# Last product of a two-layer trunk: two of the four weight sums of a pair by DMA accumulation, five pairs by seven products

## The chip, the cores and the metric

The kernel runs on one core of one Trainium2 chip. The metric is the device time of one execution in microseconds. The core has five engines that work side by side, each through its own instruction queue in order: TensorE (PE in the profile, its weight loads PEld), VectorE (DVE), ScalarE (ACT), GpSimd (POOL) and SyncE (SP, which here only issues DMAs). Engines wait for each other by semaphores. A DMA is issued by an engine's queue and done by 16 DMA engines.

## What is computed

Two decoder layers on 256 tokens of 1024 channels. Each layer is a half-weighted SwiGLU block, an attention block and a second half-weighted SwiGLU block; a final RMSNorm closes it. Only the last SwiGLU block of layer 1 and the final norm matter here:

```
def swiglu(h, w_gate, w_up, w_down):
    return (jax.nn.silu(h @ w_gate) * (h @ w_up)) @ w_down
...
h = h + FFN_RESIDUAL_WEIGHT * swiglu(rmsnorm(h, ffn2_norm[layer]),
                                     ffn2_w_gate[layer], ffn2_w_up[layer], ffn2_w_down[layer])
...
return rmsnorm(h, final_norm)
```

`w_down` is 2816 x 1024 in float32. The last product multiplies the activations (256 tokens x 2816) by it.

## The kernel before, in words

Every float32 product is done as three matmuls of a rounded type: each operand is split into a high part (a rounded copy, made by ACT) and a low part (the rest, made by DVE as source minus high part), and `product()` (L181) issues high x high, high x low and low x high, each 128x128 against 128x512, all into one PSUM tile.

The last product is `down_last()` (L435). The 2816 rows of `w_down` are 22 blocks of 128 rows, taken as 11 pairs (0 to 10). For one pair the work is a product of two 2x2 block matrices: two blocks of tokens by two blocks of rows on the left, two blocks of rows by two halves of 512 columns on the right. An ordinary pair takes eight block products (24 matmuls). A pair whose number is in `FAST` (L29, before: 2, 4, 6, 7) takes seven (21 matmuls), by sums of blocks of the left and of the right side. `fast()` (L476) issues them in the order 1, 11, 12, 5, 7, 6, 21; the products 1, 5, 6 and 7 add up over the fast pairs in four PSUM tiles m1, m5, m6, m7, and `collect()` (L486) combines these into the output tiles `h` after the last fast pair: one ACT instruction, six of DVE and two of POOL. The pairs 9 and 10 are kept back (`tail=2`) and done output block by output block, so that each block can be finished (residual added at L524, squares and gain) while PE works on the next.

The weights of a pair come in by `load()` (L459): one DMA of 1 MB from SP's queue into a tile `raw` of four quarters, numbered 0 to 3: first row block, left and right half, then second row block, left and right half. An ordinary pair is split as it is. A fast pair needs four sums of quarters, named a, c, b and d:

- a = quarter 0 + quarter 1 and c = quarter 3 + quarter 1, both by one DVE instruction over 1024 columns into the tile `ac` (L467);
- b = a + quarter 3, by POOL (L468);
- d = b + quarter 2, by POOL (L469).

`split()` (L448) makes high and low parts in four pieces: a (quarters 0 and 2), b (quarter 3), c (the tile `ac`) and d (the sums b and d). In names of the profile `wh_f_d_8c` is the high part of piece c of pair 8, and `wl_f_d_8c` its low part. The sums of the left side of a fast pair are made one stage earlier, in `quarter_sums()` (L342), while that pair's activations are made.

What sets the order and the waits:

- `raw` has four buffers, shared by all loads of weights, so the load of pair i + 4 waits until everyone has read pair i's tile: ACT, DVE and, in a fast pair, POOL.
- The high and the low pieces have eight buffers each (`wp`), so a piece is split only when PE has used the one eight pieces back.
- The tiles `ac` use the tag `qkl` with two buffers, which the attention used before for the low parts of its queries and keys; each fast pair reuses the buffers of the fast pair two back.
- Each engine's order is fixed when the program is built, by a scheduler that places instructions by when it expects their inputs. A wait in a queue holds everything behind it on that engine, DMA issues included.

In the stage before, the gate and up products of the same SwiGLU block, POOL multiplies each `j_f_u` by the norm's row (L371), between DVE's steps L339 and L379.

Of the kernel before, what the change touches and what calls it, by code (L numbers as in the profile page):

```python
# [11 lines left out]
F32R = mybir.dt.float32r  # L12
AF = mybir.ActivationFunctionType
ALU = mybir.AluOpType

P = 128
# [9 lines left out]
NG = H // HG  # L26
ROT = 16
HALF = ROT // 2
FAST = (2, 4, 6, 7)  # L29
LEAD = 4  # L30
EPS = 1e-6
SCALE = DH ** -0.5
# [34 lines left out]
def trunk(ctx: ExitStack, tc: tile.TileContext, a: dict, out: bass.AP):  # L67
    nc = tc.nc
# [7 lines left out]
    pp = ctx.enter_context(tc.tile_pool(name="pp", bufs=2))  # L76
# [101 lines left out]
    def rows(w, k0, k, c0, n):  # L178
        return w[k0 * P:(k0 + k) * P, c0:c0 + n].rearrange("(k p) n -> p k n", p=P)
# [255 lines left out]
    def down_last(name, w, blocks, sums, h, weight, part, after, tail=2):  # L435
# [12 lines left out]
        def split(n, *srcs):  # L448
            k = sum(src.shape[1] for src in srcs)
            wh, wl = [wp.tile([P, k, 512], F32R, tag=tag, name=f"{tag}_{name}_{n}") for tag in ("wh", "wl")]  # L450
            at = 0
            for src in srcs:
                part = slice(at, at + src.shape[1])
                nc.scalar.activation(wh[:, part], src, AF.Copy)
                nc.vector.tensor_sub(wl[:, part], src, wh[:, part].bitcast(F32))
                at = part.stop
            return [(wh[:, i, :], wl[:, i, :]) for i in range(k)]

        def load(i):  # L459
            raw = rawp.tile([P, 4, 512], F32, tag="raw", name=f"raw_{name}_{i}")  # L460
            nc.sync.dma_start(raw.rearrange("p (k c) n -> p k (c n)", k=2), rows(w, 2 * i, 2, 0, D))
            if i not in sums:
                return split(f"{i}a", raw[:, :2]) + split(f"{i}b", raw[:, 2:])
            n = 2 * (sorted(sums).index(i) % 4)
            ac = ap_.tile([P, 2, 512], F32, tag="qkl", name=f"sum_{name}_{i}ac", bufs=2)
            b, d = [xp.tile([P, 1, 512], F32, tag=f"x{n + j}", name=f"sum_{name}_{i}{'bd'[j]}") for j in range(2)]
            nc.vector.tensor_add(ac, raw[:, 0::3], raw[:, 1:2].to_broadcast([P, 2, 512]))  # L467
            nc.gpsimd.tensor_tensor(b[:, 0], ac[:, 0], raw[:, 3], op=ALU.add)  # L468
            nc.gpsimd.tensor_tensor(d[:, 0], b[:, 0], raw[:, 2], op=ALU.add)  # L469
            b11, b21 = split(f"{i}a", raw[:, 0::2])  # L470
            b22, = split(f"{i}b", raw[:, 3:])
            ta, tc = split(f"{i}c", ac)
            tb, td = split(f"{i}d", b, d)
            return b11, b21, b22, ta, tc, tb, td
# [24 lines left out]
        quarters = [[("11", c11), ("12", c12)], [("21", c21), ("22", c22)]]  # L499
        pairs = KF // 2  # L500
        ahead, held = [load(0)], []
        for i in range(pairs):
            if i + 1 < pairs:
                ahead.append(load(i + 1))
            ws = ahead.pop(0)
            if i in sums:
                fast(i, ws)
                if i == max(sums):
                    collect()
            elif i < pairs - tail:  # L510
                for k in range(2):
                    for t in range(NT):
                        for c in range(2):
                            add(*quarters[t][c], blocks[t][2 * i + k], ws[2 * k + c])
            else:
                held += [(2 * i + k, ws[2 * k:2 * k + 2]) for k in range(2)]
        end = acc(f"dn_{name}_end")[:, :S]
        for t in range(NT):
            for c in range(2):
                n, ac = quarters[t][c]  # L520
# [232 lines left out]
    w, n = a["a_w_qkv"][0], HG * DH  # L753
# [25 lines left out]
    sums = {}  # L779
    for n, i in enumerate(FAST):  # L780
        if n < 2:
            sums[i] = tuple(xp.tile([P, 512], F32R, tag=f"kx{4 + 2 * n + j}", name=f"left_{i}_{j}") for j in range(2))
        else:
            parts = ap_.tile([P, 2, 512], F32R, tag="qkh", name=f"left_{i}", bufs=2)
            sums[i] = (parts[:, 0], parts[:, 1])
# [78 lines left out]
```

## Time and profile before

| | us |
|---|---|
| median of three runs | 986.85 (986.69 to 988.29) |
| the profiled execution | 986.84 |
| span of its trace | 985.1 |
| PE busy in the span | 972.6 |
| DVE busy | 753.1 |
| ACT busy | 594.7 |
| POOL busy | 213.1 |
| last product on PE, first to last matmul | 921.5 to 979.0 |

In the rows of a timeline the columns are start and length in us, the engine, the line of the kernel, the operation, output and inputs by the program's names (leading numbers in names are left out), the shape, the count, and in brackets how long the engine stood idle before and which engine's instruction ended that. A group's row gives the least, the median and the longest duration in ns and the first and last start. The matmuls' lengths are modelled; the distance from one start to the next, 0.227 us for 128x512, is what PE takes for each. SPq, ACTq and POOLq are the queues' own instructions, such as DMA issues.

### The profile page before, as it was taken

Reading aid. Unit: us, or ns where it says so; the run is one execution under the profiler, and the core shown is the slowest. Engines: PE = TensorE matmul, PEld = TensorE weight load, DVE = VectorE, ACT = ScalarE, POOL = GpSimd, SP = SyncE. Lnnn points to the kernel's source line nnn. Section 1 sums busy time; section 2 is a strip of 40 time slices with the busy share of each in tenths; the row PEclk is TensorE's granted clock in tenths of the full one; section 3 lists DMA queues with packets and bytes.
Section 4 is the critical chain, followed back from the end, with each engine's and each line's share of the span. In section 5 each row is a group of like instructions: output and inputs, shape, how many; then the busy total and the mean of one; then the engine's idle time right before and its main releaser. Section 6 shows DMA issues by size and latency. Waiting matters only on the chain.

```text
span 985.1 us, 15279 instructions
## 1 busy us (share of the span) xinstructions
PE 972.6 (99%) x5640; PEld 847.2 (86%) x5640; DVE 753.1 (76%) x1313; ACT 594.7 (60%) x1090; POOL 213.1 (22%) x220
## 2 busy tenths in 40 slices
PE   8999999999999999999999999999999999999997
PEld 5888888888889888888888888888888998888886
DVE  7987866677877788776668887657677778888996
ACT  7666654457776665654456556544577766666561
POOL 3211111122332211110112111111042422112461
PEclk9999999999999999999999999999999999999999
DMA  9876565655443556555655565665544255565351
GB/s 317 256 242 208 161 210 186 214 172 166 133 130 107 181 187 203 178 198 189 213 173 172 185 200 184 200 196 192 197 132 140 90 168 164 180 200 184 128 172 43
DMA packets 152251, 176.03 MB, mean 179 GB/s; under 512 B 3440, under 2 KB 140144, under 8 KB 152176
## 3 DMA queue, kind: packets, MB, share of 16 engines
q1 hardware_dynamic: 151328, 174.01, 55.1%
q8 instruction: 44, 0.72, 0.3%
q10 hardware_dynamic: 848, 1.05, 0.3%
q14 instruction: 31, 0.25, 0.1%
HBM read 173.99 MB, written 1.05 MB: 178 GB/s over the span
## 4 chain that ended last, share of the span: by engine, by line
PE 68%; ACT 2%; DVE 2%; issue 1%; POOL 0%; POOLq 0%; ACTq 0%; DVEq 0%
PE f_g L195 12%; PE f_u L195 12%; PE dn_f L195 8%; PE f_u L198 6%; PE f_g L198 6%; PE dn_f L198 4%; PE dn_f_d L184 1%; PE dn_f_d L186 1%; PE dn_f_d L188 1%; PE q_b L184 1%; PE kv_b L184 1%; PE q_b L188 1%; PE kv_b L188 1%; PE q_b L186 1%; PE kv_b L186 1%; PE ot_ao L546 1%
## 5 line engine op out<-in xcount | busy, mean ns | idle before, releaser
L195 PE MATMUL f_g<-x_n,wh_f_g 128*128 128x512 f32 x688 | 180.4, 394 | 0.0
L195 PE MATMUL f_u<-x_n,wh_f_u 128*128 128x512 f32 x688 | 177.3, 390 | 0.0
L371 POOL TENSOR_TENSOR j_f_u<-j_f_u,r_n 128x256 f32<-128x256 f32 x88 | 80.5, 917 | 376.2 <-DVE j_f_u L339 352.7
L195 PEld LDWEIGHTS f_u<-x_n,wh_f_u 128*128 128x128 f32 x688 | 129.2, 188 | 27.3
L195 PEld LDWEIGHTS f_g<-x_n,wh_f_g 128*128 128x128 f32 x688 | 124.0, 189 | 22.7
L195 PE MATMUL dn_f<-act_f,wh_f 128*128 128x512 f32 x528 | 126.5, 391 | 0.0
L159 DVE TENSOR_TENSOR wl_f_u<-raw_f_u,wh_f_u 128x1024 fp32r<-128x1024 f32 x86 | 118.5, 1380 | 2.9 <-ACT wh_f_u L158 2.8
L159 DVE TENSOR_TENSOR wl_f_g<-raw_f_g,wh_f_g 128x1024 fp32r<-128x1024 f32 x86 | 103.5, 1233 | 15.7 <-PE f_g L198 9.3
L195 PEld LDWEIGHTS dn_f<-act_f,wh_f 128*128 128x128 f32 x528 | 96.9, 188 | 18.6
L159 DVE TENSOR_TENSOR wl_f<-raw_f,wh_f 128x1024 fp32r<-128x1024 f32 x72 | 81.8, 1153 | 36.0 <-ACT wh_f L158 26.8
L198 PE MATMUL f_u<-x_n,wl_f_u 128*128 128x256 f32 x688 | 103.3, 283 | 0.0
L198 PE MATMUL f_g<-x_n,wl_f_g 128*128 128x256 f32 x688 | 102.7, 282 | 0.0
L198 PEld LDWEIGHTS f_g<-x_n,wl_f_g 128*128 128x128 f32 x688 | 96.4, 190 | 6.2
L158 ACT ACTIVATE wh_f<-raw_f 128x1024 fp32r<-128x1024 f32 x72 | 67.3, 978 | 49.5 <-PE dn_f L195 27.2
L158 ACT ACTIVATE wh_f_u<-raw_f_u 128x1024 fp32r<-128x1024 f32 x86 | 86.7, 1048 | 16.7 <-PE f_g L195 10.9
L158 ACT ACTIVATE wh_f_g<-raw_f_g 128x1024 fp32r<-128x1024 f32 x86 | 89.5, 1048 | 9.8 <-issue 6.0
L198 PEld LDWEIGHTS f_u<-x_n,wl_f_u 128*128 128x128 f32 x688 | 91.6, 192 | 0.0
L232 POOL TENSOR_TENSOR ss_n<-ss_n,sq_n 128x256 f32<-128x256 f32 x42 | 41.8, 996 | 221.6 <-ACT sq_n L231 220.7
L369 ACT ACTIVATE j_f_g<-j_f_g 128x256 f32<-128x256 f32 x88 | 36.7, 417 | 66.2 <-DVE j_f_g L368 65.8
L98 ACT ACTIVATE act_f<-j_f_g 128x256 fp32r<-128x256 f32 x80 | 33.0, 417 | 65.4 <-DVE j_f_g L379 65.3
L198 PEld LDWEIGHTS dn_f<-act_f,wl_f 128*128 128x128 f32 x528 | 68.1, 191 | 2.8
L198 PE MATMUL dn_f<-act_f,wl_f 128*128 128x256 f32 x528 | 69.0, 283 | 0.0
(553 smaller groups left out, 1795.8 us busy)
## 6 DMA issues: line engine op xcount, KB each, us to landing
raw_f_g<-in_ffn_w_gate_dram SPq DMA_DIRECT2D x43, 1024.0 KB, 5.4
raw_f_u<-in_ffn_w_up_dram SPq DMA_DIRECT2D x43, 1024.0 KB, 5.4
raw_f<-in_ffn_w_down_dram SPq DMA_DIRECT2D x24, 1024.0 KB, 5.2
raw_f_d<-in_ffn_w_down_dram SPq DMA_DIRECT2D x11, 1024.0 KB, 5.0
raw_f<-in_ffn_w_down_dram SPq DMA_DIRECT2D x12, 768.0 KB, 4.5
raw_qka<-in_a_w_qkv_dram SPq DMA_DIRECT2D x16, 512.0 KB, 4.3
raw_va<-in_a_w_qkv_dram SPq DMA_DIRECT2D x4, 1024.0 KB, 5.2
raw_ao<-in_a_w_o_dram SPq DMA_DIRECT2D x4, 1024.0 KB, 5.0
```

What stands on the lines that cost most here:

```text
L98: nc.scalar.activation(hi, src, AF.Copy, scale=scale)
L158: nc.scalar.activation(wh, r, AF.Copy)
L159: nc.vector.tensor_sub(wl, r, wh.bitcast(F32))
L184: nc.tensor.matmul(ac, xh, wh, start=first, stop=False)
L186: nc.tensor.matmul(ac, xh, wl, start=False, stop=False)
L188: nc.tensor.matmul(ac, xl, wh, start=False, stop=last)
L195: nc.tensor.matmul(ac, wh, flat(x), start=first and i == 0, stop=False)
L198: nc.tensor.matmul(ac[:, :S], wl, x[:, 0, :], start=False, stop=last and i == len(ws) - 1)
L232: nc.gpsimd.tensor_tensor(self.ss, self.ss, sq, op=ALU.add)
L369: nc.scalar.activation(g, g, AF.Silu)
L371: nc.gpsimd.tensor_tensor(u, u, norm.row, op=ALU.mult)
L546: nc.tensor.matmul(ac, wl[:, d], hi, start=False, stop=k == KD - 1 and j == 1)
```

## The change

The list of fast pairs becomes 2, 4, 5, 7, 8: 6 becomes an ordinary pair, 5 and 8 become fast ones. The sums a and c are no longer made by DVE. SP loads the quarters 0 and 3 a second time from DRAM, straight into `ac` (two DMAs of 256 KB), and a DMA from GpSimd's queue adds quarter 1, out of `raw`, to both halves of `ac` (512 KB, source and destination in SBUF). POOL's sums b and d, and the splits, stay as they are, and wait for that DMA. `collect()` follows pair 8 instead of pair 7. The left sums of the fifth fast pair get a tile of their own in a pool that the attention used.

```diff
-FAST = (2, 4, 6, 7)
+FAST = (2, 4, 5, 7, 8)
...
-            nc.vector.tensor_add(ac, raw[:, 0::3], raw[:, 1:2].to_broadcast([P, 2, 512]))
+            src = w[2 * i * P:(2 * i + 2) * P, :].rearrange("(k p) (c n) -> p k c n", p=P, c=2)
+            for k in range(2):
+                nc.sync.dma_start(ac[:, k], src[:, k, k])
+            nc.gpsimd.dma_start(ac, raw[:, 1:2].to_broadcast([P, 2, 512]), accum_op=ALU.add)
             nc.gpsimd.tensor_tensor(b[:, 0], ac[:, 0], raw[:, 3], op=ALU.add)
             nc.gpsimd.tensor_tensor(d[:, 0], b[:, 0], raw[:, 2], op=ALU.add)
...
+        elif n == 4:
+            sums[i] = tuple(pp.tile([P, 512], F32R, tag="pT", name=f"left_{i}_{j}") for j in range(2))
```

In the program as built, the order of the instructions around the change is this. On SP the loads into `ac` of pairs 2 and 4 stand in the first part of the gate and up stage, long before their pairs; those of pair 5 stand behind the raw load of pair 6, those of pair 7 behind raw 8, those of pair 8 behind raw 9. On POOL the addition for pair 2 stands between the products of `j_f_u` 17 and 18, that for pair 4 between 19 and 20; those for 5, 7 and 8 each stand right before b and d of their own pair. On ACT and DVE the pieces follow each other in the order of the pairs.

## The prediction

> **What bounds the kernel now.** I read the page first, then the stage of the last product in the windows view, then the timelines of its engines.
>
> ```profile
> span 985.1 us, 15279 instructions
> PE 972.6 (99%) x5640; PEld 847.2 (86%) x5640; DVE 753.1 (76%) x1313; ACT 594.7 (60%) x1090; POOL 213.1 (22%) x220
> ```
> ```profile
> 880.00:900.00 20.00, 20.00 (x120) 17.81 (x119) 16.83 (x32) 12.36 (x24) 3.29 (x4) 1.00 0.63 205
> 930.00:940.00 10.00, 10.00 (x46) 8.29 (x45) 10.00 (x13) 7.13 (x9) 5.70 (x1) 1.00 0.45 162
> 940.00:950.00 10.00, 10.00 (x46) 8.29 (x45) 9.12 (x8) 5.46 (x7) 9.84 (x4) 1.00 0.66 206
> ```
>
> The columns of the second fence are the stretch, its length, then busy time of PE, PEld, DVE, ACT and POOL, the granted clock, DMA share and GB/s. PE is never idle in the last product, at full clock. So PE work taken out is time won, provided nothing that feeds PE becomes late. But DVE is full too (10.00 and 9.12 of 10), and DVE and POOL make what PE eats. The timeline of PE prices the two kinds of pair; the rows are the first matmuls of pairs 2, 3, 8 and 9:
>
> ```profile
> 932.40 0.39 PE L184 MATMUL dn_f_d_m<-wh_f_d_2a,act_f 128*128 128x512 f32 x1
> ```
> ```profile
> 937.16 0.39 PE L184 MATMUL dn_f_d<-wh_f_d_3a,act_f 128*128 128x512 f32 x1
> ```
> ```profile
> 962.33 0.39 PE L184 MATMUL dn_f_d<-wh_f_d_8a,act_f 128*128 128x512 f32 x1
> ```
> ```profile
> 967.76 0.39 PE L184 MATMUL dn_f_d<-wh_f_d_9a,act_f 128*128 128x512 f32 x1
> ```
>
> A pair of seven products lasts 937.16 - 932.40 = 4.76 us (21 matmuls, 0.227 us apart); one of eight lasts 967.76 - 962.33 = 5.43 us.
>
> **The change, part by part.**
>
> *One more pair by seven products.* Three matmuls go: 3 x 0.227 = 0.68 us. This is the only term that can make the kernel faster. Pairs 0 to 4 and 6, 7 start as before (5 saves what 6 gives back); pair 8 still starts at 962.33 and ends at 967.09.
>
> *The sums on DVE.* Removed are four instructions of 1.22 us, the fourth like these three, 4.87 us together:
>
> ```profile
> L467 DVE TENSOR_TENSOR sum_f_d_2ac<-raw_f_d x1: 1214/1214/1214, 907.3 to 907.3; 128x1024 f32<-128x1024 f32 x1
> L467 DVE TENSOR_TENSOR sum_f_d_4ac<-raw_f_d x1: 1218/1218/1218, 917.9 to 917.9; 128x1024 f32<-128x1024 f32 x1
> L467 DVE TENSOR_TENSOR sum_f_d_6ac<-raw_f_d x1: 1218/1218/1218, 933.0 to 933.0; 128x1024 f32<-128x1024 f32 x1
> ```
>
> A fifth pair splits seven quarters of 512 columns instead of four: by the two split rows further down (1.21 for 1024 columns, 0.68 for 512) 2 x 1.21 + 3 x 0.68 = 4.46 us of DVE instead of 2.42, so 2.0 more; ACT likewise about 1.9 more, beside its 2.9 and 4.5 us idle in 10. Its left side has sums of its own, in the stage before:
>
> ```profile
> L347 DVE TENSOR_TENSOR q_f<-act_f x4: 410/412/417, 838.1 to 894.6; 128x256 f32<-128x256 f32 x4
> L348 DVE TENSOR_TENSOR q_f<-q_f,act_f x4: 276/284/292, 838.6 to 895.3; 128x128 f32<-128x128 f32 x4
> L349 DVE TENSOR_TENSOR q_f<-act_f,q_f x4: 279/280/282, 839.1 to 895.8; 128x128 f32<-128x128 f32 x4
> L94 DVE TENSOR_TENSOR left<-q_f,left x4: 682/688/692, 840.1 to 897.6; 128x512 fp32r<-128x512 f32 x4
> ```
>
> The left sums add 0.41 + 0.28 + 0.28 + 0.69 = 1.66 us of DVE before 905 us, where DVE had 3.17 us idle in 20 (first windows row): cost 0; without that idle time, at most 1.66. In the last product DVE is relieved by 4.87 - 2.0 = 2.8 us. It is not what PE waits for, so this buys no time by itself; it is cover. POOL gets two more adds and five issues.
>
> *The plain loads on SP.* Ten loads of 256 KB come in. Those of pairs 2 and 4 stand far ahead in SP's queue, behind the second gate load of this layer half, and wait for the last reader of the tiles `qkl`, the scores of the second attention:
>
> ```profile
> 757.20 0.37 SPq L148 DMA_DIRECT2D raw_f_g<-in_ffn_w_gate_dram  x1
> 767.03 0.37 SPq L148 DMA_DIRECT2D raw_f_u<-in_ffn_w_up_dram  x1
> ```
> ```profile
> 765.94 0.39 PE L597 MATMUL s_b<-qkh_b,qkl_b 64*128 64x256 f32 x2
> ```
>
> The scores end at 766.3, before SP's next load at 767.03, so nothing behind them is held: cost 0 (if it were held, by less than 1 us, 140 us ahead of need). The loads for 5, 7 and 8 stand late, between the raw loads 6 to 10. These must not wait long, and by the chain below raw 9 waits for POOL's last sum of pair 5, at 942; raw 10 stands behind it and behind the loads of pair 8. PE uses both from 967.1, and a 1 MB load lands in 5.0 (row below): cover of some 15 us, cost 0.
>
> *The additions on GpSimd's queue.* This is the heart. An issue on POOL waits for two landings; then b waits for the sum, d for b, and only then comes the next issue, since POOL works in order. ACT's and DVE's splits c and d of that pair wait for it too, and in their queues stand all later splits. For pairs 2 and 4 the issues fall between POOL's products j_f_u of the stage before, near 907 and 918, where DVE's sums stood; the next product waits for the issue alone, and the pairs are used at 932 and 943. Cover: over 10 us. For 5, 7 and 8 there is a serial chain of three times (addition L, b, d). Its price in rows, POOL's timeline first:
>
> ```profile
> 920.90 1.30 POOL L468 TENSOR_TENSOR sum_f_d_2b<-sum_f_d_2ac,raw_f_d 128x512 f32<-128x512 f32 x1 [0.55 <-PE f_u L198]
> 922.16 1.47 POOL L468 TENSOR_TENSOR sum_f_d_4b<-sum_f_d_4ac,raw_f_d 128x512 f32<-128x512 f32 x1
> 923.58 2.28 POOL L469 TENSOR_TENSOR sum_f_d_2d<-sum_f_d_2b,raw_f_d 128x512 f32<-128x512 f32 x1
> 925.82 1.73 POOL L469 TENSOR_TENSOR sum_f_d_4d<-sum_f_d_4b,raw_f_d 128x512 f32<-128x512 f32 x1
> ...
> 934.30 11.38 POOL L468 TENSOR_TENSOR sum_f_d_6b<-sum_f_d_6ac,raw_f_d 128x512 f32<-128x512 f32 x1 [4.40 <-DVE sum_f_d_6ac L467]
> 945.76 2.15 POOL L469 TENSOR_TENSOR sum_f_d_6d<-sum_f_d_6b,raw_f_d 128x512 f32<-128x512 f32 x1
> 947.87 1.75 POOL L468 TENSOR_TENSOR sum_f_d_7b<-sum_f_d_7ac,raw_f_d 128x512 f32<-128x512 f32 x1
> 949.70 1.62 POOL L469 TENSOR_TENSOR sum_f_d_7d<-sum_f_d_7b,raw_f_d 128x512 f32<-128x512 f32 x1
> ```
>
> Without 6b the seven have a mean of 1.76 us, so b + d = 3.5 us. 6b lasted 11.38 us while DVE was full (10.00 of 10 above) and ended in DVE's first gap: POOL's adds starve beside a full DVE. An addition by DMA doesn't occur in this trace. The nearest rows:
>
> ```profile
> raw_f_d<-in_ffn_w_down_dram SPq DMA_DIRECT2D x11, 1024.0 KB, 5.0
> ```
> ```profile
> raw_qka<-in_a_w_qkv_dram SPq DMA_DIRECT2D x16, 512.0 KB, 4.3
> ```
> ```profile
> out_dram<-out SPq DMA_DIRECT2D x2, 256.0 KB, 2.1
> ```
>
> (size, then us from issue to landing). From below L is 2.1 us, the shortest landing. From above it is an issue that starves like 6b and then lands like 1 MB: 11.4 + 5.0 = 16.4 us. I take 5.0, the row of 1 MB, because a sum fetches 512 KB from each of two places. The Trainium skill ("DMA: Bandwidth & Descriptors", Anatomy of one DMA) gives 2.0 us + bytes / 436 GB/s for this queue; as an estimate that is 3.2 us for 512 KB, with which the chain would end at 953.7. No run yet shows it.
>
> Start of the chain: pair 5's loads take pair 2's buffer when DVE has split 2c.
>
> ```profile
> 928.09 1.21 DVE L455 TENSOR_TENSOR wl_f_d_2c<-sum_f_d_2ac,wh_f_d_2c 128x1024 fp32r<-128x1024 f32 x1
> ```
>
> 929.3 + 4.3 (512 KB) = 933.6. Then T8, the end of POOL's last add of pair 8, is 933.6 + 3 x (5.0 + 3.5) = **959.1**.
>
> *What T8 must meet.* After it come a split on ACT and DVE, four splits of pairs 9 and 10 on DVE, and collect(), which moves from behind pair 7 to behind pair 8:
>
> ```profile
> 953.62 0.62 ACT L454 ACTIVATE wh_f_d_7d<-sum_f_d_7d 128x512 fp32r<-128x512 f32 x1
> ```
> ```profile
> 954.67 0.68 DVE L455 TENSOR_TENSOR wl_f_d_7d<-sum_f_d_7d,wh_f_d_7d 128x512 fp32r<-128x512 f32 x1
> ```
> ```profile
> 962.25 1.21 DVE L455 TENSOR_TENSOR wl_f_d_10b<-raw_f_d,wh_f_d_10b 128x1024 fp32r<-128x1024 f32 x1
> 963.39 0.68 DVE L490 SCALAR_TENSOR_TENSOR co_f_d_b<-dn_f_d_m,co_f_d_a 128x512 f32<-128x512 f32 x1
> ```
> ```profile
> 967.36 0.68 DVE L497 TENSOR_TENSOR h<-h,co_f_d_d 128x512 f32<-128x512 f32 x1
> ```
> ```profile
> 970.75 0.69 DVE L524 SCALAR_TENSOR_TENSOR h<-dn_f_d,h 128x512 f32<-128x512 f32 x1 [2.71 <-PE dn_f_d L188]
> ```
> ```profile
> 973.47 0.69 DVE L524 SCALAR_TENSOR_TENSOR h<-dn_f_d,h 128x512 f32<-128x512 f32 x1 [1.30 <-PE dn_f_d L188]
> ```
>
> A split steps by 963.39 - 962.25 = 1.14 us, collect takes 968.04 - 963.39 = 4.65. So collect ends at T8 + 0.62 + 0.68 + 4 x 1.14 + 4.65 = T8 + 10.5. It may end as late as the second L524, moved forward by 0.68, minus the first L524 and its output step, which DVE had done by 973.47 - 1.30 = 972.17, so in 1.42: 973.47 - 0.68 - 1.42 = 971.4. Hence T8 must be by **960.9**; PE itself would wait only from 963.3 (10b is used at 967.09 + 9 x 0.227 = 969.1, and ready at T8 + 5.9). Collect has a floor of its own: the last matmul of m6, the 18th of pair 8, starts at 966.2, lasts 0.39 and ends near 966.6, and 966.6 + 4.65 = 971.25, just in time.
>
> Sum: 959.1 is 1.8 us ahead of 960.9, so the cover holds and the 0.68 us come through: the profiled execution's 986.84 (span 985.1 and 1.74 around it; the median of three runs, 986.85, is the same) becomes **986.2**. But the cover is gone at L = 5.6, and from there each microsecond of L costs three.
>
> **The rivals.**
>
> *The chain of POOL is late (slower).* Mechanism: L above 5.6, since the raw loads share the DMA engines (share 0.45 to 0.66) and the issue itself takes POOL time. Time = 986.2 + 3 x (L - 5.6): 987.4 at 6, even with before at 5.8, 991.9 at 7.5. For it: nothing overlaps in the chain. Against it: 512 KB alone land in 4.3.
>
> *One add or issue starves as 6b did (slower).* T8 grows by 11.38 - 1.76 = 9.6 to 968.7, 7.8 late: 994.0. For it: it has happened once among eight adds. Against it: DVE has lost the four sums, and by the middle of the product it should wait for buffers and leave gaps. The Trainium skill ("SBUF — State Buffer", Who interferes with whom) has the rule: a DVE instruction with two SBUF inputs shuts out a GpSimd one that reads SBUF, not one that only writes; 6b agrees. The same page warns (SBUF: two separate sides) that DVE in a two-port mode keeps GpSimd from writing a DMA's descriptors, so that the DMA seems blocked; if that held beside these splits, the issues would starve too and the time would be this rival's, and by the first rule only adds would. No run yet shows it.
>
> *It gives nothing.* L near 5.8, or collect's floor missed by some tenths since it now ends 0.15 us before it is needed: 986.8.
>
> **How the numbers follow.** Cover holds, 986.2: 0.38. Nothing gained, or up to 988.6 (L 5.6 to 6.4): 0.18. Late chain from there to L = 8: 0.24, up to 993.4. A starved step, about 994: 0.12. Far later, L of 9 and more: 0.06. Faster by over 2 us: 0.02, since no row holds more than 0.68. The forecast's own range is 985.9 to 986.8. The whole range is 985.9 to 994.0: it leaves out the far case, half of the starved one and a little below. A measurement of this kernel tells about 0.2% (2 us) from no change. Faster beyond that 0.02; within it 0.38 + 0.18 = 0.56; slower 0.42.
>
> **What would show it.** Right: POOL's issue-to-landing of the five additions at 5 us or less, its last add of pair 8 before 961, no wait of PE between 921 and 968, pair 9 begun at 967.1, collect begun at 966.6. Late chain: landings over 5.6, ACT and DVE waiting for GpSimd's queue in pairs 5, 7 and 8, PE waiting for 7d, 8c or 8d. Starved: one POOL add of many microseconds beside a full DVE. Wrong at the root: a longer stage before 921, or raw 9 or 10 landing after PE wants them.

## The result, and the profile after

The changed kernel takes 1002.11 us (median of four runs, 999.92 to 1003.03), the kernel before 986.98 us beside it: a ratio of 1.0146, 95% interval 1.013 to 1.0162. It is 15.1 us slower where 0.7 us less were forecast. The profiled execution of the changed kernel took 1001.53 us.

The page of the changed kernel, to be held against the first lines of the prediction:

```profile
span 999.8 us, 15333 instructions
PE 978.1 (98%) x5637; PEld 848.2 (85%) x5637; DVE 752.3 (75%) x1316; ACT 596.1 (60%) x1094; POOL 211.3 (21%) x227
```

DVE's busy time has hardly moved (753.1 to 752.3 us) and PE's has grown by 5.5 (972.6 to 978.1), but the span has grown by 14.7 us: most of that is waiting. POOL's timeline shows which:

```profile
937.25 1.21 POOL L470 DMA_DIRECT2D sum_f_d_5ac<-raw_f_d  x1 [5.46 <-DVE wl_f_d_4a L455]
948.01 1.29 POOL L471 TENSOR_TENSOR sum_f_d_5b<-sum_f_d_5ac,raw_f_d 128x512 f32<-128x512 f32 x1 [9.55 <-DMA sum_f_d_5ac<-raw_f_d]
949.38 2.19 POOL L472 TENSOR_TENSOR sum_f_d_5d<-sum_f_d_5b,raw_f_d 128x512 f32<-128x512 f32 x1
951.51 1.21 POOL L470 DMA_DIRECT2D sum_f_d_7ac<-raw_f_d  x1
962.60 1.26 POOL L471 TENSOR_TENSOR sum_f_d_7b<-sum_f_d_7ac,raw_f_d 128x512 f32<-128x512 f32 x1 [9.88 <-DMA sum_f_d_7ac<-raw_f_d]
963.93 2.14 POOL L472 TENSOR_TENSOR sum_f_d_7d<-sum_f_d_7b,raw_f_d 128x512 f32<-128x512 f32 x1
966.02 1.20 POOL L470 DMA_DIRECT2D sum_f_d_8ac<-raw_f_d  x1
971.68 1.26 POOL L471 TENSOR_TENSOR sum_f_d_8b<-sum_f_d_8ac,raw_f_d 128x512 f32<-128x512 f32 x1 [4.46 <-DMA sum_f_d_8ac<-raw_f_d]
973.02 2.18 POOL L472 TENSOR_TENSOR sum_f_d_8d<-sum_f_d_8b,raw_f_d 128x512 f32<-128x512 f32 x1
```

This is the serial chain that the prediction drew: addition, b, d, and only then the next addition. T8, the end of POOL's last add of pair 8, is 973.02 + 2.18 = 975.2. The DMA issues give the landings (KB, then us from issue to landing):

```profile
sum_f_d_2ac<-raw_f_d POOLq DMA_DIRECT2D x1, 512.0 KB, 7.3
sum_f_d_4ac<-raw_f_d POOLq DMA_DIRECT2D x1, 512.0 KB, 6.1
sum_f_d_5ac<-in_ffn_w_down_dram SPq DMA_DIRECT2D x2, 256.0 KB, 6.1
sum_f_d_5ac<-raw_f_d POOLq DMA_DIRECT2D x1, 512.0 KB, 10.6
sum_f_d_7ac<-raw_f_d POOLq DMA_DIRECT2D x1, 512.0 KB, 10.9
sum_f_d_8ac<-raw_f_d POOLq DMA_DIRECT2D x1, 512.0 KB, 5.6
```

The additions for pairs 5 and 7 take twice as long as that for pair 8. SP's timeline says what they stand beside:

```profile
928.88 0.37 SPq L461 DMA_DIRECT2D raw_f_d<-in_ffn_w_down_dram  x1
930.01 0.81 SPq L469 DMA_DIRECT2D sum_f_d_5ac<-in_ffn_w_down_dram  x2
936.09 2.17 SPq L461 DMA_DIRECT2D raw_f_d<-in_ffn_w_down_dram  x2
938.96 0.87 SPq L469 DMA_DIRECT2D sum_f_d_7ac<-in_ffn_w_down_dram  x2
951.59 0.38 SPq L461 DMA_DIRECT2D raw_f_d<-in_ffn_w_down_dram  x1
952.13 0.83 SPq L469 DMA_DIRECT2D sum_f_d_8ac<-in_ffn_w_down_dram  x2
955.60 0.38 SPq L461 DMA_DIRECT2D raw_f_d<-in_ffn_w_down_dram  x1
```

Pair 5's addition (issued at 937.25) shares the DMA engines with raw 7 and 8 (936.09 and on) and pair 7's loads into `ac`, 2.5 MB; pair 7's (951.51) with raw 9, pair 8's loads and raw 10. The latter is no accident: raw 9 takes pair 5's buffer, whose last reader is 5d, the same instruction behind which POOL issues the next addition. The windows view over the three landings (DMA share and GB/s are the last two columns):

```profile
937.20:948.00 10.80, 10.80 (x49) 8.94 (x48) 4.67 (x6) 1.38 (x2) 1.21 (x1) 1.00 0.99 283
951.50:962.50 11.00, 10.01 (x41) 7.09 (x39) 5.41 (x6) 4.00 (x5) 1.22 (x2) 1.00 0.91 250
966.00:971.70 5.70, 5.21 (x19) 3.87 (x17) 3.15 (x4) 2.10 (x3) 1.24 (x3) 0.83 0.55 95
```

In the first two the DMA engines are busy 99% and 91% of the time, in the third 55%. DVE, which was full before, now works 4.67 us of 10.80 in the first of them. What comes behind T8 is DVE's queue (splits of 9 and 10, collect(), then the output blocks):

```profile
980.26 2.32 DVE L455 TENSOR_TENSOR wl_f_d_10b<-raw_f_d,wh_f_d_10b 128x1024 fp32r<-128x1024 f32 x1
982.50 0.68 DVE L493 SCALAR_TENSOR_TENSOR co_f_d_b<-dn_f_d_m,co_f_d_a 128x512 f32<-128x512 f32 x1
986.47 0.68 DVE L500 TENSOR_TENSOR h<-h,co_f_d_d 128x512 f32<-128x512 f32 x1
988.39 0.68 DVE L527 SCALAR_TENSOR_TENSOR h<-dn_f_d,h 128x512 f32<-128x512 f32 x1
```

collect() ends at 987.15, that is T8 + 11.95. The second L527 starts at 988.39, 14.9 us behind its counterpart of before at 973.47, and the span has grown by 14.7. So the end hangs on T8, which the runs below test.

### The profile page after: what moved, and what is told of

It reads as the page before. It is cut to its first block, busy times and chain, and to the rows that moved or that the text cites. A ratio compares the mean times of both kernels' runs of the same rounds, so it can differ in the third digit from the quotient of the medians.

```text
span 999.8 us, 15333 instructions
## 1 busy us (share of the span) xinstructions
PE 978.1 (98%) x5637; PEld 848.2 (85%) x5637; DVE 752.3 (75%) x1316; ACT 596.1 (60%) x1094; POOL 211.3 (21%) x227
## 4 chain that ended last, share of the span: by engine, by line
PE 63%; DVE 3%; DMA 2%; ACT 2%; issue 2%; POOL 1%; POOLq 0%; ACTq 0%; DVEq 0%
PE f_g L195 12%; PE f_u L195 12%; PE dn_f L195 8%; PE f_u L198 6%; PE f_g L198 6%; PE dn_f L198 4%; DMA sum_f_d_7ac<-raw_f_d 1%; DMA sum_f_d_5ac<-raw_f_d 1%; PE q_b L184 1%; PE kv_b L184 1%; PE q_b L188 1%; PE kv_b L188 1%; PE q_b L186 1%; PE kv_b L186 1%; PE ot_ao L549 1%
## 5 line engine op out<-in xcount | busy, mean ns | idle before, releaser
L195 PE MATMUL f_g<-x_n,wh_f_g 128*128 128x512 f32 x688 | 180.4, 394 | 0.0
L195 PE MATMUL f_u<-x_n,wh_f_u 128*128 128x512 f32 x688 | 177.3, 390 | 0.0
L195 PEld LDWEIGHTS f_u<-x_n,wh_f_u 128*128 128x128 f32 x688 | 129.2, 188 | 27.3
L195 PEld LDWEIGHTS f_g<-x_n,wh_f_g 128*128 128x128 f32 x688 | 124.0, 189 | 22.7
L195 PE MATMUL dn_f<-act_f,wh_f 128*128 128x512 f32 x528 | 126.5, 391 | 0.0
L195 PEld LDWEIGHTS dn_f<-act_f,wh_f 128*128 128x128 f32 x528 | 96.9, 188 | 18.6
L158 ACT ACTIVATE wh_f<-raw_f 128x1024 fp32r<-128x1024 f32 x72 | 67.3, 978 | 49.4 <-PE dn_f L195 27.1
L158 ACT ACTIVATE wh_f_u<-raw_f_u 128x1024 fp32r<-128x1024 f32 x86 | 86.7, 1048 | 16.7 <-PE f_g L195 10.9
L158 ACT ACTIVATE wh_f_g<-raw_f_g 128x1024 fp32r<-128x1024 f32 x86 | 89.5, 1048 | 10.3 <-issue 6.0
```

The costliest lines, as they stand in the source:

```text
L158: nc.scalar.activation(wh, r, AF.Copy)
L195: nc.tensor.matmul(ac, wh, flat(x), start=first and i == 0, stop=False)
```

## Experiments

The theory to be tested: T8 sets the time, and T8 is late mainly because the additions share the DMA engines with the raw loads. Rivals: the addition is slow by itself; the fifth pair or the later collect() makes the loss; every addition costs its landing, chain or not.

### The fifth pair without the additions

```diff
-            for k in range(2):
-                nc.sync.dma_start(ac[:, k], src[:, k, k])
-            nc.gpsimd.dma_start(ac, raw[:, 1:2].to_broadcast([P, 2, 512]), accum_op=ALU.add)
+            nc.vector.tensor_add(ac, raw[:, 0::3], raw[:, 1:2].to_broadcast([P, 2, 512]))
```

> Five pairs by seven products (2, 4, 5, 7, 8), but all sums a and c on DVE as before; no load into the tile ac, nothing on GpSimd's queue. If the additions by DMA made the loss (theories: they share the DMA engines with the raw loads; or they are slow by themselves), the fifth pair alone comes out at 986.2 to 987, at most 0.7 us under the kernel before. If the fifth pair or the later collect() made it, the time is near 1002. Rival for a small loss: DVE has 2.0 + 1.2 us more to do in a stretch where it was full, up to 3.2 us, 990.

Measured: 986.99 us against 987.06, ratio 0.9999 (0.999 to 1.0008). The fifth pair makes no loss; but its 0.68 us don't arrive either. The last row of PE, first of this kernel, then of before:

```profile
977.90 0.28 PE L188 MATMUL dn_f_d_end<-wh_f_d_10b,act_f 128*128 128x256 f32 x1
```
```profile
978.68 0.28 PE L188 MATMUL dn_f_d_end<-wh_f_d_10b,act_f 128*128 128x256 f32 x1
```

PE is through 0.78 us earlier. DVE is not; windows, then DVE's timeline of this kernel:

```profile
950.00:960.00 10.00, 10.00 (x46) 8.28 (x45) 10.00 (x8) 7.91 (x12) 5.03 (x3) 1.00 0.46 168
960.00:970.00 10.00, 10.00 (x46) 8.29 (x45) 9.93 (x13) 3.65 (x5) 4.98 (x2) 1.00 0.01 2
```
```profile
967.68 0.68 DVE L490 SCALAR_TENSOR_TENSOR co_f_d_b<-dn_f_d_m,co_f_d_a 128x512 f32<-128x512 f32 x1
971.65 0.68 DVE L497 TENSOR_TENSOR h<-h,co_f_d_d 128x512 f32<-128x512 f32 x1
973.58 0.68 DVE L524 SCALAR_TENSOR_TENSOR h<-dn_f_d,h 128x512 f32<-128x512 f32 x1
```

collect() begins at 967.68, some 1.1 us after the last product is there (966.6 by the prediction's count), because DVE is still at the splits, and the second L524 falls at 973.58 where before had 973.47. What PE saved, DVE lost: by the prediction's count the fifth pair gives it 2.0 us more of splits, and a sum of 1.2. That DVE's queue is the cause is read off this trace; the tries further down that relieved DVE did not bring the gain.

### The additions without the fifth pair

```diff
-FAST = (2, 4, 5, 7, 8)
+FAST = (2, 4, 6, 7)
```

> The four pairs of before (2, 4, 6, 7) with the additions by DMA. Theory that the chain of GpSimd's additions is what costs: only two links are left behind pair 4 (6 and 7). With landings of 10 to 11 us the last add of pair 7 ends near 937.3 + 2 x 14.2 = 965.7, some 6 us after PE wants 7c, so the time is 5 to 10 us over before (992 to 997), with PE waiting for 6c or 7c. Rival, that the fifth pair or collect() made the loss: within 1 us of before.

Measured: 991.73 us, ratio 1.0046 (1.0032 to 1.0059), a loss of 4.7 us with two links behind pair 4. Landings were 10.3 and 8.5 us, and pair 7's last add ended at 962.2, not 965.7; PE waited for pieces 7c and 8a. The size is just under the range expected; the rival (no loss) falls.

### A copy in place of the addition

```diff
-            nc.gpsimd.dma_start(ac, raw[:, 1:2].to_broadcast([P, 2, 512]), accum_op=ALU.add)
+            nc.gpsimd.dma_start(ac, raw[:, 1:2].to_broadcast([P, 2, 512]))
```

> As the changed kernel, but the DMA on GpSimd's queue copies quarter 1 over the tile ac in place of adding it; so the sums a and c are left out, all else is the same order and size. If it is the adding that is slow, landings fall to 5 us or less and the time is 986 to 988. If it is the sharing of the DMA engines, landings in pairs 5 and 7 stay at 9 to 11 us and the time at 998 to 1002. Half and half (an addition keeps the engines busy for twice as long as a copy, and both wait for the raw loads): 7 to 8 us, 990 to 995.

Measured: 991.53 us, ratio 1.0044 (1.003 to 1.0057). DMA issues of this kernel:

```profile
sum_f_d_5ac<-raw_f_d POOLq DMA_DIRECT2D x1, 512.0 KB, 6.8
sum_f_d_7ac<-raw_f_d POOLq DMA_DIRECT2D x1, 512.0 KB, 8.5
sum_f_d_8ac<-raw_f_d POOLq DMA_DIRECT2D x1, 512.0 KB, 3.3
```

Half and half: the same bytes copied land in 3.3 us undisturbed, where the addition takes 5.6, and beside raw loads in 6.8 and 8.5 where it takes 10.6 and 10.9. So adding costs 2.3 us by itself, 3.8 and 2.4 under load, and a plain copy is disturbed too.

### Raw loads taken away

```diff
-            raw = rawp.tile([P, 4, 512], F32, tag="raw", name=f"raw_{name}_{i}")
-            nc.sync.dma_start(raw.rearrange("p (k c) n -> p k (c n)", k=2), rows(w, 2 * i, 2, 0, D))
+            if i < 9:
+                raw = rawp.tile([P, 4, 512], F32, tag="raw", name=f"raw_{name}_{i}")
+                nc.sync.dma_start(raw.rearrange("p (k c) n -> p k (c n)", k=2), rows(w, 2 * i, 2, 0, D))
+                kept[:] = [raw]
+            raw, = kept
```

> As the changed kernel, but the raw loads of pairs 9 and 10 are left out (these pairs use pair 8's tile), so that 2 MB less move while the addition of pair 7 is under way. Sharing of the DMA engines: the addition of pair 7 lands in 6 to 7 us instead of 10.9, that of pair 5 stays near 10.6, that of pair 8 near 5.6, and the time falls by 4 to 6 us to 996 to 998. Slow by itself, or held by its descriptors: 10 us or more for pair 7 and 1002.

> As the changed kernel, but the raw loads of pairs 7 to 10 are left out (these pairs use pair 6's tile), so that beside the addition of pair 5 only the 512 KB into the tile ac of pair 7 are left. Sharing of the DMA engines: the addition of pair 5 lands in 6 to 7 us (10.6 in the changed kernel, 8.8 with raw 9 and 10 left out), 7 and 8 in 5.5. The chain of three with landings of 6.5, 5.5 and 5.5 from 937.2 then ends near 965, still 4 us after 960.9: 990 to 992. If bare landings were all that is needed, or the chain began in time: 987 or less. If the additions are slow for another reason than the raw loads: 994 or more, with pair 5 near 9 us.

The second kernel is the first with `i < 7`. Measured: 994.58 us, ratio 1.0076 (1.0062 to 1.0089), and 991.17 us, ratio 1.0043 (1.0028 to 1.0058). The additions and POOL's last add, of the first:

```profile
sum_f_d_5ac<-raw_f_d POOLq DMA_DIRECT2D x1, 512.0 KB, 8.8
...
sum_f_d_7ac<-raw_f_d POOLq DMA_DIRECT2D x1, 512.0 KB, 5.4
sum_f_d_8ac<-raw_f_d POOLq DMA_DIRECT2D x1, 512.0 KB, 5.5
```
```profile
965.77 2.18 POOL L475 TENSOR_TENSOR sum_f_d_8d<-sum_f_d_8b,raw_f_d 128x512 f32<-128x512 f32 x1
```

and of the second, with the start of its chain:

```profile
sum_f_d_5ac<-raw_f_d POOLq DMA_DIRECT2D x1, 512.0 KB, 5.7
...
sum_f_d_7ac<-raw_f_d POOLq DMA_DIRECT2D x1, 512.0 KB, 5.5
sum_f_d_8ac<-raw_f_d POOLq DMA_DIRECT2D x1, 512.0 KB, 5.2
```
```profile
936.82 1.21 POOL L473 DMA_DIRECT2D sum_f_d_5ac<-raw_f_d  x1 [5.25 <-ACT wh_f_d_4d L454]
...
962.01 2.18 POOL L475 TENSOR_TENSOR sum_f_d_8d<-sum_f_d_8b,raw_f_d 128x512 f32<-128x512 f32 x1
```

Each addition drops to 5.2 to 5.7 us as soon as the raw loads beside it are gone, so these loads are what stretches it. That the two share the time of the DMA engines is read from the shares of 0.99 and 0.91 above; no run separates these engines from the memory that they read and write. T8 moves from 975.20 to 967.95 to 964.19, by 11.0 us in all, and the time by 10.9. The remaining 4.1 us over before belong to an undisturbed chain of three. (In the first kernel pair 5's addition took 8.8 instead of 10.6 with the same loads behind it in SP's queue; why is open.)

### One late addition in place of three

```diff
-FAST = (2, 4, 5, 7, 8)
+FAST = (2, 4, 8)
```

> Only pairs 2, 4 and 8 by seven products, their sums a and c by the DMA additions: one addition behind pair 4 in place of three, so no chain on GpSimd's queue. One pair fewer by seven products than before costs 0.68 us. Theory of the chain: the single late addition may last 10 us and still ends (with b and d) near 957, before 960.9, so the time is 0.7 us over before (0.5 to 1.5) and PE doesn't wait. Theory that every late addition costs its own landing (some 5 us each: add_four lost 4.7 with two, the change 15 with three): 5 us or more over before.

Measured: 987.9 us, ratio 1.0008 (0.9999 to 1.0017), 0.8 us over before, as the chain theory has it; PE waits nowhere in the last product. That each addition costs its landing falls. The addition was issued at 942.65 and landed in 5.4, although raw 9 was issued at 940.41 and raw 10 at 945.02. The three took turns: from 945 to 948 the DMA engines moved 174 to 215 GB/s, about what they moved for pair 8's addition alone in the changed kernel (184 to 193 from 968 to 970), and from 948 on some 400. So in this run one load issued 2 us before the addition and one issued 2 us behind it hardly lengthened it.

### Early and late additions apart

```diff
+            if i < 5:
...
+            else:
+                nc.vector.tensor_add(ac, raw[:, 0::3], raw[:, 1:2].to_broadcast([P, 2, 512]))
```

The branch that is cut holds the two loads into `ac` and the addition by DMA; the second kernel has `i >= 5`.

> Five pairs by seven products; additions by DMA for pairs 2 and 4 only, whose sums are wanted late; DVE's sums for 5, 7 and 8. No chain: landings of 6 to 7 us for 2 and 4 as in the changed kernel, hidden behind pairs 0 to 3, and the time is that of five pairs with DVE's sums alone, 986.3 to 987.5. If the additions hurt where nothing waits for them (by the DMA engines or by GpSimd's time): 989 or more.

> The counterpart of the run with additions for pairs 2 and 4 only: DVE's sums for 2 and 4, additions by DMA for 5, 7 and 8. Chain theory: the end of GpSimd's last add of pair 8 near 973 to 975, the whole loss is there: 1000 to 1002. If the additions of pairs 2 and 4 had a large part in the loss (the run with them alone lost 1.5 us against before): 998 or less.

Measured: 988.56 us, ratio 1.0017 (1.0008 to 1.0026), with the early ones; 1001.93 us, ratio 1.0146 (1.0132 to 1.016), with the late ones. The loss is in the late chain, whose T8 was 976.86. The kernel with the early ones lost 1.5 us, between the two ranges of its expectation. PE waited once in its last product:

```profile
953.50 0.50 PE L186 MATMUL dn_f_d<-wl_f_d_6a,act_f 128*128 128x512 f32 x1 [0.43 <-DVE wl_f_d_6a L455]
```

Its DVE queue is late from the end of the stage before, and POOL's timeline shows why:

```profile
926.12 1.43 POOL L474 TENSOR_TENSOR sum_f_d_4b<-sum_f_d_4ac,raw_f_d 128x512 f32<-128x512 f32 x1 [2.99 <-DMA sum_f_d_4ac<-raw_f_d]
...
931.18 0.73 POOL L371 TENSOR_TENSOR j_f_u<-j_f_u,r_n 128x256 f32<-128x256 f32 x1
```

POOL waits 2.99 us for pair 4's addition before it makes 4b, and the last product `j_f_u` stands behind that pair's sums. DVE's step L379 waits for it 1.88 us, where it waited 0.64 in the run with DVE's sums; collect() begins at 969.40 there, 1.7 us later than in that run. The run with one late addition has the same wait (1.89) and loses nothing by it; there DVE works 5.11 us of 10 from 960 to 970, where it was full in the run with five pairs and DVE's sums. The rest of the lag is not the additions': the last product began at 922.06 (before: 921.5), but PE was already 0.5 us late in the kernel's first microseconds (its first product of L195 at 7.99 instead of 7.48). The kernel with the late additions, whose last product began at 923.47, fell behind between 275 and 300 us, where the granted clock was 0.93 (before: 1.00), over 600 us ahead of the first addition.

### Half of the addition

```diff
-            for k in range(2):
-                nc.sync.dma_start(ac[:, k], src[:, k, k])
-            nc.gpsimd.dma_start(ac, raw[:, 1:2].to_broadcast([P, 2, 512]), accum_op=ALU.add)
+            nc.sync.dma_start(ac[:, 0], src[:, 0, 0])
+            nc.gpsimd.dma_start(ac[:, 0], raw[:, 1], accum_op=ALU.add)
+            nc.vector.tensor_add(ac[:, 1], raw[:, 3], raw[:, 1])
```

> As the changed kernel, but only the sum a comes by the DMA addition (one load of 256 KB into ac, one addition of 256 KB); DVE makes c over 512 columns. If an addition's landing goes by its bytes above a fixed part, the undisturbed one of pair 8 falls from 5.6 to about 4 us, those beside raw loads from 10.6 and 10.9 to 6 to 8; the last add of pair 8 ends near 965 and the time is 990 to 994. If a landing is mostly fixed (descriptors, the queue): 5 us or more for pair 8, 998 or more in all.

Measured: 990.43 us, ratio 1.003 (1.0019 to 1.0041), in the range; the eight runs spread from 988.64 to 993.28, and the profiled one took 993.13.

```profile
sum_f_d_5ac<-raw_f_d POOLq DMA_DIRECT2D x1, 256.0 KB, 7.5
...
sum_f_d_7ac<-raw_f_d POOLq DMA_DIRECT2D x1, 256.0 KB, 8.2
...
sum_f_d_8ac<-raw_f_d POOLq DMA_DIRECT2D x1, 256.0 KB, 3.4
```

Undisturbed, 256 KB take 3.4 us and 512 KB 5.6. As an estimate from these two landings, that is 2.2 us for each 256 KB above about 1.2 fixed. Beside the raw loads, 7.5 and 8.2 are in or just above the 6 to 8 that were expected.

### Three tries at a faster kernel

In the trace of the first run DVE's queue took the fifth pair's gain. Three ways to relieve it, each from that kernel (five pairs, DVE's sums):

```diff
-            nc.vector.tensor_add(h[1][0], h[1][0], c)
+            nc.gpsimd.tensor_tensor(h[1][0], h[1][0], c, op=ALU.add)
```

> Five pairs by seven products with DVE's sums, and one of collect()'s two additions to h on DVE (1.41 us) given to GpSimd. In the run with five pairs and DVE's sums PE ended 0.78 us earlier than before, but DVE, never idle from 949 to 975, began collect() at 967.7 and ended it at 972.3, 0.9 us after it was needed; the span was the same. If DVE's queue took the gain away, it comes back: 0.5 to 0.8 us under before (986.3). If something else sets the end: 987.

Measured: 987.02 us, ratio 0.9999 (0.9991 to 1.0008). The 1.41 us went from DVE, but the next addition to h on DVE stood beside GpSimd's and took 1.81 us instead of 0.68; the second L524 fell at 973.87. The gain does not come.

```diff
-FAST = (2, 4, 5, 7, 8)
+FAST = (1, 2, 4, 6, 7)
```

> Five pairs by seven products, all sums on DVE, but pairs 1, 2, 4, 6 and 7: the fifth pair stands early, where DVE had 1 to 2 us idle in 10, and collect() follows pair 7 as before. If DVE's full queue in the last third took away the gain of the fifth pair (2, 4, 5, 7, 8 with DVE's sums came out even with before), the 0.68 us now come through: 986.2 to 986.5. If DVE is too full everywhere from 905 on, or the fifth pair's left sums delay the stage before: 987 or more.

Measured: 988.41 us, ratio 1.0009 (1.0 to 1.0017): none either. PE waited 1.47 us for the low part of piece 2a, which stood on DVE behind a step that waited 1.88 us for a product j_f_u, queued on POOL behind the sums of pairs 1, 2 and 4.

```diff
+            if i == 8:
...
+            else:
+                nc.vector.tensor_add(ac, raw[:, 0::3], raw[:, 1:2].to_broadcast([P, 2, 512]))
```

> Five pairs by seven products (2, 4, 5, 7, 8), DVE's sums for 2, 4, 5 and 7, the addition by DMA for pair 8 alone: no chain, and DVE is rid of one sum of 1.22 us in the stretch where it was never idle. GpSimd issues the addition behind 7d near 950.6; raw 9 and 10 have landed by then except perhaps the last. With a landing of 5.5 to 8 us the last add of pair 8 ends at 959.5 to 962. If DVE's queue is what took the gain of the fifth pair, and the single addition is in time: 986.2 to 986.7, faster than both kernels. If the raw loads stand beside it (10 us) the last add ends at 964 and the wait goes on to collect(): 988 to 990. If neither moves the end: 987.

Measured: 989.66 us, ratio 1.0026 (1.0015 to 1.0038). The addition landed in 5.5 (2 us behind raw 10, issued at 952.07), but was issued at 954.04 instead of 950.6: its loads into `ac`, at 946.85, landed in 6.0. T8 was 963.17, and the wait went on to collect(). No kernel here is measurably faster than before.

## Why the prediction was wrong

**The step that failed is the price of the addition, L = 5.0 us**, with which T8 was 959.1. T8 came at 975.2, 16.1 us later. By terms: the three landings were 10.6 + 10.9 + 5.6 = 27.1 instead of 15.0, 12.1 us; the chain began at 937.25 instead of 933.6, 3.65 us; b, d and the hand-over took 37.95 - 27.1 = 10.85 instead of 10.5, 0.35 us. (37.95 is 975.20 - 937.25.) L is the largest part but not the only one: with L = 5.0 the chain from 937.25 would have ended at 937.25 + 25.5 = 962.75, still past the 959.7 that was needed (both terms are below).

- *Why L was wrong.* 5.0 was a landing by itself, and as that it was near (5.2 to 5.7). The prediction listed the sharing as a rival's mechanism ("the raw loads share the DMA engines") and did not work out how many bytes are in flight beside each addition, though it had placed raw 9 behind POOL's last sum of pair 5. The runs without raw loads show it: 11.0 us of T8. The upper bound of 16.4 held each landing; the range's top of 994.0 took in L up to 8.
- *The start.* The prediction has 929.3 + 4.3. The loads into `ac` were issued at 930.01, since DVE's split 2c took 1.98 us instead of 1.21 and ended at 929.94. They landed in 6.1 instead of 4.3, beside raw 6 (issued at 928.88). The addition followed 1.1 us behind that landing, a step that the prediction left out.
- *The cover.* With the start of the undisturbed run, 936.82, and collect() ending at T8 + 11.95 instead of T8 + 10.5 (split 10b took 2.32 us beside POOL's addition to h), the chain would have to have L under 5.6 - (3.2 + 1.45) / 3 = 4.05. No addition of 512 KB reached that: 5.2 was the shortest. So the change would have lost even with L nearly as predicted, and did (991.17). The Trainium skill ("DMA: Bandwidth & Descriptors", Anatomy of one DMA) gave 3.2 us as an estimate; the copy's 3.3 agrees, the addition's 5.2 to 5.7 does not.
- *The mechanism* was right: the rival of the late chain, to which the prediction gave 0.24, and 0.06 to landings of 9 us and more; their mean was 9.0. ACT and DVE waited for GpSimd's queue in pairs 5, 7 and 8. That T8 sets the end held in each kernel whose chain was late. Profiled time minus T8:

| kernel | T8 | profiled execution | difference |
|---|---|---|---|
| the changed one | 975.20 | 1001.53 | 26.33 |
| raw 9, 10 out | 967.95 | 994.39 | 26.44 |
| raw 7 to 10 out | 964.19 | 990.81 | 26.62 |
| copy | 965.16 | 991.53 | 26.37 |
| half | 966.49 | 993.13 | 26.64 |
| late three | 976.86 | 1003.51 | 26.65 |
| eight alone | 963.17 | 989.51 | 26.34 |

  With 986.2 as the best, T8 had to be by about 959.7, not 960.9.
- *Three matmuls fewer, 0.68 us:* right for PE (0.78 us in the first run, 0.8 us lost with one pair fewer), but by the traces it reaches the end only if DVE is free for collect(), which held in no run with five pairs; that it would come through then is not shown.
- *The early additions at nothing:* pairs 2 and 4 had landings of 7.3 and 6.1 us, above 5.0 too, and for PE their cover held: its first wait in the changed kernel's last product is for piece 5c, at 950.48. That "the next product waits for the issue alone" did not hold: POOL waited 2.93 us for pair 4's landing before 4b, the last product `j_f_u` stood behind, and DVE waited 1.89 us for it. In the changed kernel the late chain hides this; in the run with early additions alone it shows.
- *The plain loads at nothing:* right for the early ones. Those of pair 5 set the start of the chain (above). Those of 7 and 8 and raw 9, 10 came in time for their own readers and cost by what they did to the additions. The wait that was placed rightly (raw 9 behind 5d) was read only for what it delays, not for what it starts.
- *No starving of adds or issues:* right. Issues took 1.20 to 1.39 us, adds 1.26 to 2.27, beside a DVE with gaps. With DVE's sums the starved add was there again (5b, 10.23 us in the first run).

## What to carry to other kernels

A DMA's landing read off a trace holds for what moved beside it; before a transfer goes on a serial path, list the loads that the same event releases and add their bytes. A chain on an in-order queue multiplies each error by its links: three late additions cost 15 us; a single one cost nothing when it was issued at 942.65, and 2.5 us when it was issued at 954.04, past its cover. And work taken from the engine that sets the pace is only won if the engine that feeds and empties it has the time for what the change adds there.

## What the runs showed of the hardware

An addition by DMA, 512 KB within SBUF, takes 5.2 to 5.7 us undisturbed against 3.3 for a copy of the same bytes. It takes 8.5 beside one load of 1 MB issued with it (the run with two links, issued at 950.06 and 950.14), and 8.8 to 10.9 beside 2.5 MB of loads issued about when it is.

After two waits of PE close together the matmuls come at a wider distance for some 2 us; PE's timeline of the changed kernel:

```profile
963.71 0.50 PE L184 MATMUL dn_f_d_m<-wh_f_d_7c,left 128*128 128x512 f32 x1 [1.63 <-ACT wh_f_d_7c L454]
965.00 0.80 PE L186 MATMUL dn_f_d_m<-wl_f_d_7c,left 128*128 128x512 f32 x1 [0.78 <-DVE wl_f_d_7c L455]
965.59 0.63 PE L188 MATMUL dn_f_d_m<-wh_f_d_7c,left 128*128 128x512 f32 x1
966.02 0.63 PE L184 MATMUL dn_f_d_m<-wh_f_d_7c,left 128*128 128x512 f32 x1
```

From 965.59 to 967.72 they start 0.43 us apart, and from 968.06 on 0.23 again; the granted clock was 0.50 over 965.59 to 967.72. The same followed the waits of 1.65 and 0.76 us for piece 8c (0.51 over 974.69 to 978.02). It did not follow a single wait of 1.47 us in the run with the early fifth pair, nor waits of 0.53 and 0.76 us for piece 8c with raw 9 and 10 left out: the clock stayed at 1.00. The Trainium skill ("TensorE: Matmul & The Clock Gate", Wait — 56ns, not 53.3ns?) gives 426.7 ns for 512 columns at half clock, with which these rows agree. By the traces it costs nothing of its own here: behind 8d PE waits again for DVE, 1.27 us for the low part of piece 10b.
